# Gate weights' low parts on GpSimd, the scan lane at 2 steps a tick, and the last quarter of the late modulation beside the output projection

## The chip, the cores and the metric

One core of a Trainium2 chip runs the whole program. The metric is the time of one execution on the device in microseconds (us). Of the core's engines this case speaks of PE (TensorE, matmuls), DVE (VectorE), ACT (ScalarE), POOL (GpSimd) and SP (SyncE, which issues most of the DMAs).

## What is computed

One layer of a latent-token backbone: 512 tokens of width 2048, 256 context tokens, all in float32. The conditioning vector c gives six modulation rows of 2048 each, by a matrix-vector product. Cut to what this case touches:

```python
mod_lat = silu(c) @ w_mod + b_mod
sh1, sc1, g1, sh2, sc2, g2 = split(mod_lat, 6)          # six blocks of 2048
h = modulate(x, norm1_w, sh1, sc1)
z = h @ w_in                                             # 2048 -> 1024 + 1024 + 2*2048
y_a = s5_branch(z[:, :1024], ...)                        # state-space scan, readout, w_glu
y_b = pool_branch(z[:, 1024:2048], ...)
gate_a = sigmoid(z[:, 2048:4096]); gate_b = sigmoid(z[:, 4096:6144])
x = x + g1 * ((gate_a * (y_a @ proj_a) + gate_b * (y_b @ proj_b)) @ w_out)
x = x + g2 * peer_ffn(modulate(x, norm2_w, sh2, sc2), ...)
out = rmsnorm(x, final_w)
```

The state-space branch works on 64 groups of 16 channels with 64 states each; its scan over chunks of tokens is followed by a readout that multiplies the states by tables made from the parameters.

## The kernel before, in words

**Matmuls in three passes.** A float32 weight block of 128 x 1024 (a chunk) is loaded into `wraw` by SP, rounded to `whi` by ACT (L125), and the remainder `wlo = wraw - whi` is taken by DVE or GpSimd (L126, in `wload`); `mm3` then issues hi x hi, lo x hi and hi x lo (L110 to L112). The pool of `wlo` has two buffers, those of `wraw` and `whi` three. Of a matmul, `psg` is a gate's accumulator, `psp` a projection's, `psr` the readout's, `psl` the late modulation's.

**The order.** The program is written stage by stage, and a scheduler puts each engine's instructions into one fixed order by priority and by when it reckons their inputs to be there; `wload` asks for a high priority. On the chip each engine then runs its own list in order. Side work comes in through *lanes*: generators of small steps. Every `wload` ends in a `tick`, which runs so many steps of each lane as its rate says (3.4 steps a tick for a rate of 3.4). `drain` runs what is left of a lane.

**The stages around the change**, in the time of the profiled execution: the pooling branch with the first four gate_a blocks, up to 546 us; **gates** (546 to 983), 64 chunks of 24 matmuls (8 x (4 chunks of gate_b and 2 of proj_b), then 4 x 4 chunks of gate_a); **readout** and w_glu (983 to 1096); proj_a and merge (1096 to 1194); w_out (1194 to 1375); then the expert layer, with its query matmul (1394 to 1590), dense U (1590 to 2850) and dense V (2850 to 3967).

**Lanes in gates.** Three run beside the gate matmuls:
- `s5_scan` (L672 on), 86 steps of four dependent DVE instructions on 128 x 128 tiles (`sa`, `sb`, `sa`, `B`; L678 to L681) and 8 steps of three copies (L687 to L689). Readout needs all of `B`.
- `s5_m3` (L606 to L622), 32 steps of six GpSimd instructions on 128 x 256 tiles (`m`, `m3t`), each step followed by an SP DMA of the result to a table in HBM (`m3d`); every second step begins with a DMA of `par` and a GpSimd instruction `npar`. All its tiles have one buffer. Readout loads the tables, four steps to each of its eight blocks (`rm`).
- `mod_late` (L804 on), the four modulation blocks that are needed only after the merge, in 16 pieces of 512 columns (four quarters of four pieces; the fourth quarter is g2, which only the very last residual needs). A piece is 16 loads of a 128 x 512 block `lw` (256 KB each, by SP), 16 DVE instructions into `lacc` (L817, L819), then a sum over partitions on PE (`psl`, L824, recorded as a pair of matmuls), an addition on DVE (`lrow`, L825), and a GpSimd DMA into `modd` (L826). The b_mod row comes by a GpSimd DMA too (L822).

GpSimd's list in gates also holds the DMAs that write the gates' results (`mbd`, L771; `sad`, L781). In readout GpSimd multiplies `ru` (L864), eight times, ahead of `ry`, the transposes `pst` and w_glu.

Of the kernel before, what the change touches and what calls it, by code (L numbers as in the profile page):

```python
# [6 lines left out]
F32 = mybir.dt.float32  # L7
# [10 lines left out]
P = 128  # L18
# [75 lines left out]
class Builder:  # L94
# [62 lines left out]
    def body(self, es):  # L157
        tc, nc, I = self.tc, self.nc, self.I
        pool = lambda **k: tc.tile_pool(**k)
        const = es.enter_context(pool(name="const", bufs=1))  # L160
        self.const = const
        self.dram = es.enter_context(pool(name="scr", bufs=1, space=DRAM))
        self.pse = pse = self.es()
        psT = [pse.enter_context(pool(name=f"psT{j}", bufs=1, space=PSUM)) for j in range(2)]
        self.psM, self.psT2 = psT[1], Turns(psT)
        self.psT = self.psT2
        self.psA = pse.enter_context(pool(name="psA", bufs=6, space=PSUM))

        def cload(name, shape, dt=F32):
            t = const.tile(shape, dt, name=name)  # L170
            nc.sync.dma_start(t, I[name])
            return t

        self.ident = cload("ident", [P, P])
        self.ones = const.tile([P, P], F32, name="ones")
        nc.vector.memset(self.ones, 1.0)
        self.epsb = const.tile([P, 1], F32, name="epsb")
        nc.vector.memset(self.epsb, EPS)
        cT = cload("cT", [P, KT, 2])
        self.bmodT = cload("bmodT", [P, 32])  # L180
        self.n1T = cload("n1T", [P, KT])
        self.sil = const.tile([P, KT, 2], F32, name="sil")
        nc.scalar.activation(self.sil, cT, AF.Silu)

        self.bgT = cload("bgT", [P, 8])
        self.kT = cload("kT", [P, 2, P])
        self.iota = cload("iota", [P, P])
        self.lanes = []
        ws = self.es()
        self.wraw = ws.enter_context(pool(name="wraw", bufs=3))  # L190
        self.wlo = ws.enter_context(pool(name="wlo", bufs=2))
        self.whi = ws.enter_context(pool(name="whi", bufs=3))
        self.mixers()
        self.tail()
        self.peer()
        ws.close()
        pse.close()
# [62 lines left out]
    def rstd(self, pool, x, junk):  # L260
        nc = self.nc
        ss = pool.tile([P, 1], F32, tag="ss", name=self.nm("ss"))
        nc.scalar.activation(junk, x, AF.Square, accum_out=ss)
        sd = pool.tile([P, 1], F32, tag="sd", name=self.nm("sd"))
        nc.scalar.activation(sd, ss, AF.Sqrt, bias=self.epsb, scale=1.0 / D)
        rs = pool.tile([P, 1], F32, tag="rs", name=self.nm("rs"))
        nc.vector.reciprocal(rs, sd)
        return rs

    def mixers(self):  # L270
        tc, nc, I = self.tc, self.nc, self.I
        pool = lambda **k: tc.tile_pool(**k)
# [107 lines left out]
        with self.es() as s6:  # L380
            yb, lane_s = self.pool_branch(s6, es_b, hlat, s5, lane_i)
            lane_m = self.lane(0.7, [self.s5_toeplitz(), self.s5_m3()])
            lane = self.lane(3.4, [self.mod_late()])
            self.gates(hlat, yb)
        es_h.close()
        self.drain(lane_s)
        self.drain(lane_m)
        self.check("gates")
        with self.es() as s7:
            gt = self.s5_readout(s7)  # L390
            self.drain(lane)
            es_b.close()
            es_m = self.es()
            m = self.merge(s7, es_m, gt)
        self.m, self.es_m = m, es_m
# [298 lines left out]
    def pool_branch(self, es, es_b, hlat, s5, lane_i):  # L694
        tc, nc, I = self.tc, self.nc, self.I
        pool = lambda **k: tc.tile_pool(**k)
# [4 lines left out]
        with self.es() as s:  # L701
            ptl = ybl
            uss = []
            for nb in range(2):
# [3 lines left out]
                for kb in range(KT // 2):  # L708
                    w = self.wchunk(I["w_in"], kb * 2, 2, W + nb * 512, 512)
# [9 lines left out]
            self.drain(lane_i)  # L719
            s5.close()  # L720
            self.scp = es_b.enter_context(pool(name="scan", bufs=2, side="right"))
            lane_s = self.lane(4, [self.s5_scan()])
            zp = s.enter_context(pool(name="zp", bufs=1, side="right"))
            wm = zp.tile([P, 4, P], F32, name="wm")
            with tc.high_priority(offset=100):
# [57 lines left out]
    def gate(self, hlat, c0):  # L783
        ps = [self.psA.tile([P, 512], F32, tag="acc", name=self.nm("psg")) for _ in range(2)]
        for kb in range(KT // 4):
            w = self.wchunk(self.I["w_in"], kb * 4, 4, c0, 256)
            for kk in range(4):
                k = kb * 4 + kk
                for j in range(2):
                    self.mm3(ps[j], w[:, kk, j * P:(j + 1) * P], hlat[:, k, :], k == 0, k == KT - 1)  # L790
        return ps

    def proj(self, wap, y, c0):
        ps = [self.psA.tile([P, 512], F32, tag="acc", name=self.nm("psp")) for _ in range(2)]
        for kb in range(2):
            w = self.wchunk(wap, kb * 4, 4, c0, 256)
            for kk in range(4):
                k = kb * 4 + kk
                for j in range(2):
                    self.mm3(ps[j], w[:, kk, j * P:(j + 1) * P], y[:, k, :], k == 0, k == 7)  # L800
        return ps


    def mod_late(self):  # L804

        nc, es = self.nc, self.es()
        lp = es.enter_context(self.tc.tile_pool(name="late", bufs=4, side="right"))
        N = 512
        for q, blk in ((0, 2), (2, 4), (1, 3), (3, 5)):
            for n in range(D // N):  # L810
                c0 = blk * D + n * N
                acc = lp.tile([P, N], F32, tag="lacc", name=self.nm("lacc"), bufs=1)
# [12 lines left out]
                nc.vector.tensor_tensor(row[:, 0], row[:, 1], ps[0:1, :], op=OP.add)  # L825
                nc.gpsimd.dma_start(self.modd[:, q * D + n * N:q * D + (n + 1) * N], row[:, 0])  # L826
                yield
        es.close()

    def brow(self, pool, ap, name):  # L830

# [5 lines left out]
    def s5_readout(self, es):  # L837
# [6 lines left out]
        gl = gp.tile([P, 8, SEQ], F32R, name="gl")  # L844
        with self.es() as s:

            s.enter_context(pool(name="pad", bufs=1)).tile([P, 4096], F32, name="pad")
            ryp = s.enter_context(pool(name="ry", bufs=2))
            rb = s.enter_context(pool(name="rb", bufs=2))
            for gb in range(NGB):  # L850
                ch = slice(gb * P, (gb + 1) * P)
                with tc.high_priority(offset=60):
                    U = rb.tile([P, GB, NCL], F32, tag="rU", name=self.nm("rU"))
                    nc.sync.dma_start(U, self.ud[:, gb * GB:(gb + 1) * GB])
                    T = rb.tile([P, Q, P], F32, tag="rT", name=self.nm("rT"))
                    nc.sync.dma_start(T, self.td[:, :, ch])
                    m3 = rb.tile([P, 4, 2, Q, H, 2], F32, tag="rm3", name=self.nm("rm3"))
                    nc.sync.dma_start(m3.rearrange("p b r s h g -> p b (r s h g)"), self.m3d[gb * 4:gb * 4 + 4].rearrange("b p n -> p b n"))
                    u = ryp.tile([NCL, Q, P], F32, tag="ru", name=self.nm("ru"))
                    nc.sync.dma_start(u, self.zs[CTX:NTOK, ch].rearrange("(c t) n -> c t n", t=Q))  # L860
                    dsk = rb.tile([NCL, P], F32, tag="rd", name=self.nm("rd"))
                    nc.sync.dma_start(dsk, I["s5_d"][0:1, ch].broadcast_to([NCL, P]))
# [533 lines left out]
```

## Time and profile before

| | us |
|---|---|
| median of three runs | 3971.0 (3961.94 to 3975.03) |
| the profiled execution | 3968.97, its span 3966.9 |
| PE busy in the span | 3750.0 (95%) |
| DVE busy | 2561.8 (65%) |
| GpSimd busy | 1761.6 (44%) |

All times in the rows are microseconds from the start of the span of that one execution; it took 2 us less than the median. PE is busy nearly everywhere, so stages are compared by what PE loses in each. In a row by stage the busy times are those of PE, PEld (weight loads), DVE, ACT and POOL, in this order. A row of a group of instructions gives their number, their busy time and mean, and the time that the engine stood idle ahead of them with what ended it.

### The profile page before, as it was taken

What the parts mean: (1) busy time and instruction counts of PE and PEld (TensorE: products, weight loads), DVE (VectorE), ACT (ScalarE), POOL (GpSimd) and SP (SyncE); (2) the same over time, 40 slices, a digit from 0 to 9 for tenths busy, and PEclk for the clock granted to TensorE, in tenths of its full rate; (3) what the DMA queues carried; (4) which work ended last, traced back from release to release, by engine and by line L of the source; (5) the groups of instructions that cost most, each with busy time, mean ns of one, the idle gap of its engine ahead of it and who ended that gap; (6) DMA issues with size and microseconds to landing.
All of it is one profiled execution on the core that took longest, in us unless ns stands there. A gap on an engine that the chain in (4) does not pass through costs nothing. (4 is left out here: it accounts for less than half of the span.)

```text
span 3966.9 us, 49308 instructions
## 1 busy us (share of the span) xinstructions
PE 3750.0 (95%) x18841; PEld 3196.8 (81%) x18841; DVE 2561.8 (65%) x3331; ACT 1187.9 (30%) x1752; POOL 1761.6 (44%) x997
## 2 busy tenths in 40 slices
PE   5999998889899899899999999999999999999997
PEld 3478876667777778799999999989977887788886
DVE  4364379996563368986767767655666666665664
ACT  4223331112222222333333333323332333333332
POOL 0043115552322323354444444446555666576652
PEclk8999999999999999999999999999999999999999
DMA  8635658789875422477877778778887877887773
GB/s 269 207 124 186 206 166 231 227 227 302 235 233 175 138 70 91 136 263 281 290 272 267 288 273 291 256 289 290 312 300 279 316 285 281 287 318 282 282 277 123
DMA packets 456382, 954.40 MB, mean 241 GB/s; under 512 B 104721, under 2 KB 248465, under 8 KB 421073
## 3 DMA queue, kind: packets, MB, share of 16 engines
q1 hardware_dynamic: 380320, 584.58, 45.5%
q0 software_dynamic: 46464, 301.03, 20.4%
q10 hardware_dynamic: 29360, 65.64, 4.5%
q8 instruction: 147, 2.41, 0.2%
q14 instruction: 91, 0.74, 0.1%
HBM read 859.88 MB, written 94.93 MB: 241 GB/s over the span
## 5 line engine op out<-in xcount | busy, mean ns | idle before, releaser
L125 ACT CAST whi<-wraw 128x1024 fp32r<-128x1024 f32 x712 | 747.2, 1051 | 1825.2 <-PE psU L111 542.1
L126 POOL TENSOR_TENSOR wlo<-wraw,whi 128x1024 fp32r<-128x1024 f32 x284 | 773.4, 2724 | 946.8 <-ACT whi L125 714.4
L126 DVE TENSOR_TENSOR wlo<-wraw,whi 128x1024 fp32r<-128x1024 f32 x428 | 595.7, 1392 | 591.9 <-ACT whi L125 341.8
L112 PE MATMUL psU<-h2Th,wlo 128*128 128x384 f32 x2048 | 693.6, 339 | 31.7 <-DVE wlo L126 20.0
L110 PE MATMUL psU<-h2Th,whi 128*128 128x384 f32 x2048 | 700.4, 342 | 6.5 <-ACT whi L125 6.5
L111 PE MATMUL psU<-h2Tl,whi 128*128 128x384 f32 x2048 | 692.5, 338 | 0.0
L111 PE MATMUL psV<-wlo,ah 128*128 128x512 f32 x1536 | 607.7, 396 | 10.0 <-POOL wlo L126 5.0
L112 PE MATMUL psV<-whi,al 128*128 128x512 f32 x1536 | 607.0, 395 | 0.0
L110 PE MATMUL psV<-whi,ah 128*128 128x512 f32 x1536 | 558.0, 396 | 9.5 <-DVE ffn L1233 5.2
L112 PEld LDWEIGHTS psU<-h2Th,wlo 128*128 128x128 f32 x2048 | 387.2, 189 | 35.9 <-issue 14.2
L1096 DVE SCALAR_TENSOR_TENSOR row<-row,h 128x2048 f32<-128x2048 f32 x128 | 340.9, 2663 | 90.2 <-DMA row<-in_u,eid 90.2
L110 PEld LDWEIGHTS psU<-h2Th,whi 128*128 128x128 f32 x2048 | 389.0, 190 | 8.4 <-ACT whi L125 8.1
L111 PEld LDWEIGHTS psU<-h2Tl,whi 128*128 128x128 f32 x2048 | 388.0, 189 | 0.0
L1089 DVE SCALAR_TENSOR_TENSOR ffn<-row,w,ffn 128x2048 f32<-128x2048 f32 x127 | 357.7, 2816 | 13.5 <-DMA row<-in_v,eid 13.5
L111 PEld LDWEIGHTS psV<-wlo,ah 128*128 128x128 f32 x1536 | 290.8, 189 | 80.7 <-POOL wlo L126 8.2
L110 PEld LDWEIGHTS psV<-whi,ah 128*128 128x128 f32 x1536 | 290.9, 189 | 77.4 <-issue 10.3
L112 PEld LDWEIGHTS psV<-whi,al 128*128 128x128 f32 x1536 | 290.3, 189 | 67.6
L1081 POOL DMA_INDIRECT row<-in_u,eid x128 | 206.2, 1611 | 249.7 <-ACT w L1097 76.6
L1144 DVE TENSOR_TENSOR oh<-io,iT 128x512 bf16<-128x512 bf16 x192 | 168.9, 920 | 193.1 <-PE psd L1152 193.0
L1081 POOL DMA_INDIRECT row<-in_v,eid x128 | 241.0, 1883 | 19.1 <-issue 6.6
L819 DVE SCALAR_TENSOR_TENSOR lacc<-lw,sil,lacc 128x512 f32<-128x512 f32 x240 | 213.6, 890 | 52.1 <-DMA lw<-in_w_mod 50.1
L112 PE MATMUL psg<-hhi,wlo 128*128 128x512 f32 x512 | 205.0, 405 | 25.9 <-DVE wlo L126 25.8
(349 smaller groups left out, 5600.4 us busy)
## 6 DMA issues: line engine op xcount, KB each, us to landing
wraw<-in_uT SPq DMA_DIRECT2D x256, 512.0 KB, 5.2
wraw<-in_v SPq DMA_DIRECT2D x256, 512.0 KB, 6.2
lw<-in_w_mod SPq DMA_DIRECT2D x256, 256.0 KB, 4.3
wraw<-in_w_in SPq DMA_DIRECT2D x96, 512.0 KB, 4.8
wmod<-in_w_mod SPq DMA_DIRECT2D x48, 512.0 KB, 5.1
sd<-sev ACTq DMA_DIRECT2D x64, 384.0 KB, 6.0
gds<-ast ACTq DMA_DIRECT2D x12, 2048.0 KB, 8.8
sr<-sd SPq DMA_DIRECT2D x32, 768.0 KB, 7.2
```

The costliest lines, as they stand in the source:

```text
L110: mm(ps, a.hi, b.hi, start=start, stop=False)
L111: mm(ps, a.hi, b.lo, start=False, stop=False)
L112: mm(ps, a.lo, b.hi, start=False, stop=stop)
L125: nc.scalar.copy(hi, raw)
L126: ins = (eng or nc.vector).tensor_tensor(lo, raw, hi.bitcast(F32), op=OP.subtract)
L819: nc.vector.scalar_tensor_tensor(acc, w, self.sil[:, k, 0:1], acc, op0=OP.mult, op1=OP.add)
L1081: nc.gpsimd.indirect_dma_start(out=r, out_offset=None, in_=I[tab], in_offset=bass.IndirectOffsetOnAxis(ap=eid[:, k:k + 1], axis=0))
L1089: V.scalar_tensor_tensor(acc, v, w, acc, op0=OP.mult, op1=OP.add)
L1096: V.scalar_tensor_tensor(u, u, 1.0, h2, op0=OP.mult, op1=OP.mult, accum_out=w[:, 0:1])
L1144: V.tensor_tensor(oh[:, q], self.io4, iT[:, q, ts].unsqueeze(1).broadcast_to([P, P, NT]), op=OP.is_equal)
```

## The change

Four edits, three of them to lanes:
1. In gates (not in the four gate_a blocks before it) `wload` is given GpSimd for the 64 subtractions `wlo`, by `self.gate_lo`.
2. The scan lane gets 2 steps a tick instead of 4.
3. `mod_late` takes a list of quarters. Three quarters run as before, at 2.6 steps a tick instead of 3.4. The fourth runs as a second generator, `late2`, in a pool of its own with two `lw` buffers instead of four, started when w_glu begins, at 1.3 a tick through w_glu, proj_a and w_out, and drained after `tail`. To make room the pad in readout shrinks.
4. Readout, which loads no weights, gets two ticks per block.

```diff
+        self.drain(self.lane_g2)
+        self.es_g2.close()
         self.peer()
...
-            lane = self.lane(3.4, [self.mod_late()])
+            lane = self.lane(2.6, [self.mod_late("late", "right", ((0, 2), (2, 4), (1, 3)))])
+            self.gate_lo = nc.gpsimd
             self.gates(hlat, yb)
+            self.gate_lo = None
...
+        self.es_g2 = self.es()
+        late2 = self.mod_late("late2", "left", ((3, 5),))
+        next(late2)
         with self.es() as s7:
             gt = self.s5_readout(s7)
             self.drain(lane)
             es_b.close()
+            self.lane_g2 = self.lane(1.3, [late2])
...
-            lane_s = self.lane(4, [self.s5_scan()])
+            lane_s = self.lane(2, [self.s5_scan()])
...
-            w = self.wchunk(self.I["w_in"], kb * 4, 4, c0, 256)
+            w = self.wchunk(self.I["w_in"], kb * 4, 4, c0, 256, self.gate_lo)
...
-            w = self.wchunk(wap, kb * 4, 4, c0, 256)
+            w = self.wchunk(wap, kb * 4, 4, c0, 256, self.gate_lo)
...
-    def mod_late(self):
-
-        nc, es = self.nc, self.es()
-        lp = es.enter_context(self.tc.tile_pool(name="late", bufs=4, side="right"))
+    def mod_late(self, name, side, parts):
+
+        nc = self.nc
+        es = self.es() if side == "right" else self.es_g2
+        lp = es.enter_context(self.tc.tile_pool(name=name, bufs=4 if side == "right" else 2, side=side))
         N = 512
-        for q, blk in ((0, 2), (2, 4), (1, 3), (3, 5)):
+        if side == "left":
+            yield
+        for q, blk in parts:
...
-            s.enter_context(pool(name="pad", bufs=1)).tile([P, 4096], F32, name="pad")
+            s.enter_context(pool(name="pad", bufs=1)).tile([P, 1536], F32, name="pad")
...
             for gb in range(NGB):
                 ch = slice(gb * P, (gb + 1) * P)
+                self.tick()
+                self.tick()
```

What it does to the lists of the engines is shown in three places. A row has the line, the operation, and what it writes and reads; lines of the changed kernel are 10 to 16 higher than those of before.

GpSimd's list in the first part of gates, before: m3 steps with a few DMAs between them.

```order
L608 TENSOR_SCALAR npar_4831<-par_805_4829 128x64
L617 TENSOR_TENSOR m3t_4834<-pm_4380,par_805_4829 128x256
L616 TENSOR_TENSOR m_807_4833<-pm_4380,par_805_4829 128x256
L619 TENSOR_TENSOR m_807_4833<-pm_4380,npar_4831 128x256
L618 TENSOR_TENSOR m_807_4833<-m_807_4833,m3t_4834 128x256
L826 DMA modd<-lrow_4979 16x1x32
L620 TENSOR_TENSOR m3t_4834<-pm_4380,par_805_4829 128x256
L621 TENSOR_TENSOR m_807_4833<-m_807_4833,m3t_4834 128x256
L771 DMA mbd<-sg_5095 128x512
```

The same place in the changed kernel:

```order
L630 TENSOR_TENSOR m3t_4818<-pm_4341,par_762_4700 128x256
L631 TENSOR_TENSOR m_788_4817<-m_788_4817,m3t_4818 128x256
L126 TENSOR_TENSOR wlo_5351<-wraw_5349,whi_5350 128x1024
L781 DMA mbd<-sg_5279 128x512
L781 DMA mbd<-sg_5283 128x512
L618 TENSOR_SCALAR npar_4876<-par_799_4874 128x64
L627 TENSOR_TENSOR m3t_4879<-pm_4341,par_799_4874 128x256
L126 TENSOR_TENSOR wlo_5406<-wraw_5404,whi_5405 128x1024
L626 TENSOR_TENSOR m_801_4878<-pm_4341,par_799_4874 128x256
L629 TENSOR_TENSOR m_801_4878<-pm_4341,npar_4876 128x256
L628 TENSOR_TENSOR m_801_4878<-m_801_4878,m3t_4879 128x256
L126 TENSOR_TENSOR wlo_5467<-wraw_5465,whi_5466 128x1024
```

A wlo stands after every two or three m3 instructions, behind whatever mbd, modd and npar stand ahead of it.

DVE's list between the third and the fourth psl, before: lacc, scan and wlo in turn.

```order
L819 SCALAR_TENSOR_TENSOR lacc_5366<-lw_5373,sil,lacc_5366 128x512
L678 TENSOR_TENSOR sa_4958<-ar_256,B 128x128
L679 TENSOR_TENSOR sb_4959<-ai_257,B 128x128
L126 TENSOR_TENSOR wlo_5556<-wraw_5554,whi_5555 128x1024
L819 SCALAR_TENSOR_TENSOR lacc_5366<-lw_5432,sil,lacc_5366 128x512
L680 TENSOR_TENSOR sa_4958<-sa_4958,sb_4959 128x128
L819 SCALAR_TENSOR_TENSOR lacc_5366<-lw_5435,sil,lacc_5366 128x512
L681 TENSOR_TENSOR B<-B,sa_4958 128x128
L819 SCALAR_TENSOR_TENSOR lacc_5366<-lw_5438,sil,lacc_5366 128x512
```

Just ahead of the third psl in the changed kernel:

```order
L832 SCALAR_TENSOR_TENSOR lacc_5011<-lw_5322,sil,lacc_5011 128x512
L690 TENSOR_TENSOR sa_5661<-sa_5661,sb_5662 128x128
L832 SCALAR_TENSOR_TENSOR lacc_5011<-lw_5367,sil,lacc_5011 128x512
L691 TENSOR_TENSOR B<-B,sa_5661 128x128
L688 TENSOR_TENSOR sa_5715<-ar_256,B 128x128
L689 TENSOR_TENSOR sb_5716<-ai_257,B 128x128
L690 TENSOR_TENSOR sa_5715<-sa_5715,sb_5716 128x128
L691 TENSOR_TENSOR B<-B,sa_5715 128x128
```

The wlo are gone. The second lacc row is the last of its piece; behind it five whole scan steps stand one after the other before the next lrow.

GpSimd's list at the end of gates and the start of readout, in the changed kernel:

```order
L631 TENSOR_TENSOR m_1155_6509<-m_1155_6509,m3t_6510 128x256
L618 TENSOR_SCALAR npar_6628<-par_1181_6626 128x64
L627 TENSOR_TENSOR m3t_6631<-pm_6446,par_1181_6626 128x256
L626 TENSOR_TENSOR m_1183_6630<-pm_6446,par_1181_6626 128x256
L629 TENSOR_TENSOR m_1183_6630<-pm_6446,npar_6628 128x256
L628 TENSOR_TENSOR m_1183_6630<-m_1183_6630,m3t_6631 128x256
L835 DMA lrow_8889<-in_b_mod 1x16x32
L791 DMA sad<-sg_7755 128x512
L630 TENSOR_TENSOR m3t_6631<-pm_6446,par_1181_6626 128x256
L791 DMA sad<-sg_7758 128x512
L880 TENSOR_TENSOR ru_7807<-ru_7807,rd_7809 64x1024
L880 TENSOR_TENSOR ru_7874<-ru_7874,rd_7876 64x1024
```

Before, the eight ru (L864) stand there one after the other, right behind the last two sad:

```order
L781 DMA sad<-sg_7920 128x512
L781 DMA sad<-sg_7923 128x512
L864 TENSOR_TENSOR ru_7950<-ru_7950,rd_7952 64x1024
L864 TENSOR_TENSOR ru_8002<-ru_8002,rd_8004 64x1024
L864 TENSOR_TENSOR ru_8054<-ru_8054,rd_8056 64x1024
```

The last steps of m3, which before end well ahead of the end of gates, now reach into readout, ahead of ru and between them.

## Rows read from the trace of the kernel before

**Rows 1.** Busy time by stage: stretch, length, engines with instructions, granted clock, DMA share, GB/s.

```profile
546.00:983.00 437.00, 388.01 (x1561) 296.91 (x1559) 387.59 (x655) 81.89 (x92) 203.24 (x257) 0.95 0.83 244
983.00:1096.00 113.00, 100.12 (x626) 87.05 (x625) 59.22 (x73) 29.61 (x37) 34.34 (x20) 0.92 0.82 238
1096.00:1194.00 98.00, 95.04 (x407) 74.86 (x406) 65.63 (x81) 28.49 (x37) 29.65 (x19) 1.00 0.72 234
1194.00:1375.00 181.00, 180.22 (x772) 143.82 (x770) 56.18 (x55) 43.73 (x60) 46.77 (x42) 1.00 0.47 158
```

**Rows 2.** Timeline of PE, two matmuls 17 apart: start, duration, engine, line, operation.

```profile
945.82 0.39 PE L112 MATMUL psg<-hhi,wlo 128*128 128x512 f32 x1
...
949.67 0.39 PE L111 MATMUL psg<-hlow,whi 128*128 128x512 f32 x1
```

**Rows 3.** Timeline of PE, the first, seventh and tenth psl.

```profile
585.51 1.87 PE L824 MATMUL psl<-lacc,ones 128*1 128x512 f32 x2 [3.54 <-DVE lacc L819]
...
804.28 1.86 PE L824 MATMUL psl<-lacc,ones 128*1 128x512 f32 x2
...
924.07 1.02 PE L824 MATMUL psl<-lacc,ones 128*1 128x512 f32 x2 [0.50 <-DVE lacc L819]
```

**Rows 4.** Waits of PE in gates: us in total, times, longest.

```profile
PE psg L112 <- DVE wlo L126: 25.8, 15, 5.6
```

**Rows 5.** DVE's groups in gates; of the scan's four lines the longest and shortest.

```profile
L819 DVE SCALAR_TENSOR_TENSOR lacc<-lw,sil,lacc 128x512 f32<-128x512 f32 x185 | 165.5, 895 | 35.1 <-DMA lw<-in_w_mod 33.9
L126 DVE TENSOR_TENSOR wlo<-wraw,whi 128x1024 fp32r<-128x1024 f32 x64 | 83.2, 1299 | 4.9 <-ACT whi L125 4.2 <-PE psg L112 0.6
L678 DVE TENSOR_TENSOR sa<-ar,B 128x128 f32<-128x128 f32 x84 | 38.6, 459 | 1.0
...
L679 DVE TENSOR_TENSOR sb<-ai,B 128x128 f32<-128x128 f32 x84 | 28.0, 333 | 0.0
```

**Rows 6.** Timeline of DVE in gates, with GpSimd busy (two) and without (three).

```profile
651.41 1.19 DVE L819 SCALAR_TENSOR_TENSOR lacc<-lw,sil,lacc 128x512 f32<-128x512 f32 x1
652.52 0.82 DVE L678 TENSOR_TENSOR sa<-ar,B 128x128 f32<-128x128 f32 x1
...
655.86 0.74 DVE L819 SCALAR_TENSOR_TENSOR lacc<-lw,sil,lacc 128x512 f32<-128x512 f32 x1
656.52 0.28 DVE L681 TENSOR_TENSOR B<-B,sa 128x128 f32<-128x128 f32 x1
656.73 0.74 DVE L819 SCALAR_TENSOR_TENSOR lacc<-lw,sil,lacc 128x512 f32<-128x512 f32 x1
```

**Rows 7.** Timeline of GpSimd at the same time.

```profile
651.42 0.64 POOL L620 TENSOR_TENSOR m3t<-pm,par 128x256 f32<-128x256 f32 x1
652.13 1.07 POOL L621 TENSOR_TENSOR m<-m,m3t 128x256 f32<-128x256 f32 x1
```

**Rows 8.** GpSimd's groups in gates; of m3's six lines the longest and shortest.

```profile
L621 POOL TENSOR_TENSOR m<-m,m3t 128x256 f32<-128x256 f32 x32 | 31.6, 989 | 2.5
...
L617 POOL TENSOR_TENSOR m3t<-pm,par 128x256 f32<-128x256 f32 x32 | 24.4, 764 | 1.0
```

**Rows 9.** GpSimd's groups in the query matmul (1394 to 1590 us).

```profile
L126 POOL TENSOR_TENSOR wlo<-wraw,whi 128x1024 fp32r<-128x1024 f32 x28 | 67.5, 2409 | 129.2 <-PE psq L112 129.2
```

**Rows 10.** Timeline of GpSimd and DVE in dense U, around two wlo of DVE.

```profile
1668.61 3.31 POOL L126 TENSOR_TENSOR wlo<-wraw,whi 128x1024 fp32r<-128x1024 f32 x1 [1.38 <-ACT whi L125]
1669.58 3.43 DVE L126 TENSOR_TENSOR wlo<-wraw,whi 128x1024 fp32r<-128x1024 f32 x1
...
1679.40 1.22 DVE L126 TENSOR_TENSOR wlo<-wraw,whi 128x1024 fp32r<-128x1024 f32 x1
```

**Rows 11.** Waits of GpSimd in gates: us in total, times, longest.

```profile
POOL npar L608 <- DMA par<-in_s5bc: 78.8, 16, 13.2
POOL m L616 <- DMA m3d<-m: 45.4, 18, 5.7
POOL modd L826 <- DVE lrow L825: 34.2, 8, 14.2
```

More of the change, by code (lines that the diff above doesn't have):

```diff
@@ L268, in rstd @@
         return rs
+    gate_lo = None
     def mixers(self):
@@ L827, in mod_late @@
                 yield
-        es.close()
+        if side == "right":
+            es.close()
     def brow(self, pool, ap, name):
```

## The prediction

> **What bounds the kernel now.** I read the busy time of each engine by stage first [rows 1]. The change touches the gates stage (546 to 983 us) and the three stages behind it. In gates PE is busy 388 of 437 us and DVE 388 too, at a granted clock of 0.95. In the two matmul stages that receive the moved quarter PE is full (95 of 98, 180 of 181) while DVE has room (66 and 56 us busy). So the one place with something to win is gates: what PE loses there.
>
> PE's own floor in gates: full-rate matmuls start 17 apart in 3.85 us, 0.2265 us each [rows 2]; a weight chunk has 24 of them, 5.45 us, and 64 chunks need 349 us. With 12 pairs of psl (about 1 us a pair, 1.9 at a lower clock [rows 3]) that is some 362 us of 437. The remaining 75 us are what a perfect change could give. PE's waits name wlo on DVE, 25.8 us ahead of psg alone [rows 4]. So DVE decides, or rather where DVE is in its fixed order when PE asks for a wlo or a lacc.
>
> Why DVE is full: the lines of DVE in gates [rows 5] beside single instructions [rows 6]. A lacc step takes 0.74 us when nothing is beside it and 895 ns on the mean; a scan instruction 0.28 undisturbed and about 0.40 on the mean of its four lines (333 to 459 ns, 337 instructions). At 651 to 653 us the cause is visible [rows 6, 7]: lacc takes 1.19, sa 0.82 and GpSimd's m 1.07 (0.64 for the instruction ahead of it), ending one after the other. DVE and GpSimd hold each other up when both read two SBUF tiles. The sum: 185 x 0.155 + 337 x 0.12 + 64 x 0.08 = 29 + 40 + 5 = 74 us, caused by 192 m3 instructions (six lines of 32, the dearest and the cheapest in [rows 8]): **0.385 us of DVE per m3 instruction**, 60% of its undisturbed 0.64.
>
> **The change part by part.**
>
> *Low parts to GpSimd.* DVE loses 64 wlo of 1.22 us. GpSimd gets them at 2.41 us each where it runs beside little else [rows 9]: 154 us on an engine that is busy 203 of 437. Some 40 of the m3 instructions (0.76 to 0.99 us over the six lines, about 0.86 [rows 8]) then come after the last wlo, so its total in gates is about 203 + 154 - 40 x 0.86 = 323 us: not the bound by itself. What a wlo on GpSimd costs DVE is not to be seen in gates before; the nearest row is in dense U, where one on GpSimd from 1668.61 stretches DVE's wlo from 1.22 to 3.43 us [rows 10]: 2.2 us when DVE has work waiting. The low bound is the share that m3 costs, 60% of 2.41, 1.4 us. Both are more than the 1.15 to 1.22 that DVE saves. A lower price is not excluded where DVE idles; that is the first rival. I take 1.75 us for the first part of the stage, where DVE is hardly ever without work.
>
> The Trainium skill ("SBUF — State Buffer", section "Who interferes with whom") speaks against this part: a DVE instruction with two SBUF inputs and a GpSimd instruction that reads SBUF exclude each other for the whole instruction. The 3.43 us row agrees. By that rule at full price (2.41 a wlo, 0.64 an m3) step 2 below would take 275 us instead of 240; the gates' 0.385 per m3 says that only some of it reaches DVE.
>
> *The scan lane, 4 to 2 steps a tick.* The rate falls, but the order of DVE does not spread: the scan's last copy stands before the seventh psl now, and stood behind the ninth before. Between psl 1 and psl 7 there are now 66 scan steps (264 instructions) and 24 copies where there were 55 steps and 1 copy, beside the same 96 lacc steps. So the room that the wlo leave is filled with scan, early, and the end of the stage is empty for DVE.
>
> *The last quarter.* psl 1 to 12 lay in gates before, 1 to 10 do now: 2 x 16 lacc steps of 0.74 to 0.9, about 26 us of DVE, leave the end of gates, and their lw loads (0.25 MB each) a stretch with a DMA share of 0.83.
>
> *The sum by psl marks*, since PE waits there for DVE in order. Before: psl 1 at 585.5, psl 7 at 804.3, psl 10 at 924.1 us [rows 3].
> 1. To psl 1: 6 to 7 wlo hold DVE for 9 to 14 us, and its own queue is 2 us shorter: 592 to 600, I take 596.
> 2. psl 1 to 7 (29.2 chunks; PE alone 29.2 x 5.45 + 6 = 165). DVE undisturbed: a lacc to the next start 0.66, a scan instruction 0.21, more where it needs the one ahead, mean 0.27 [rows 6]; 96 x 0.66 + 264 x 0.27 + 24 copies and 14 small additions at about 0.5 = 63 + 71 + 20 = 154. Locks: 79 m3 x 0.385 = 30; 29 wlo x 1.4 to 2.2 = 41 to 64. Waits for lw: 0 to 17 (half of the 33.9 in [rows 5]). Together 225 to 265; I take 240. The same working for before gives 63 + 220 x 0.27 + 30 wlo x 1.15 + 10 + 37 for half of the m3 + 17 = 221, against 218.8 measured.
> 3. psl 7 to 10 (12.8 chunks): DVE 41 + 13 wlo x 1.4 to 2.2 + 27 m3 x 0.385 = 69 to 80; PE 73. I take 77.
> 4. psl 10 to the end (15.5 chunks): PE 84.5; GpSimd 16 x 2.41 + 36 m3 x 0.86 + 13 small ones at 0.6 = 77, nearly as much, before any wait. I take 92 (85 to 100).
>
> Sum 596 + 240 + 77 + 92 = 1005, against 983: **gates +22** (-8 to +64).
>
> *GpSimd's queue* is in order, and now wlo stand behind m3, modd and npar, and PE behind wlo. Before, m waited 45.4 us for m3d (18 times), npar 78.8 for par (16), modd 34.2 for DVE's lrow (8), with nobody urgent behind them [rows 11]. Two wlo buffers give a lead of one chunk, 5.45 us, of which the wlo itself takes 2.4, so a wait of over 3 us just ahead of a wlo shows on PE. Where DVE sets the pace (8 us a chunk in step 2) there is room for it; in step 4 there is not, which is why I take 92 there. The rest is a rival.
>
> *Readout.* About 40 m3 instructions stand ahead of, and between, the eight ru. The first ru waits for some 14 of them, 12 us after the last wlo. PE has the first block's psr and part of the next first (about 45 short matmuls, 10 us), so 0 to 3 us show; the last blocks' m3 are hidden under w_glu matmuls that now stand among the psr groups. With that cover gone it would be 40 x 0.86 = 34 us. psl 11 to 13 and two extra ticks a block fill some of PE's gaps (13 of 113 us). Net 0 (-8 to +12).
>
> *proj_a and w_out.* psl 15 and 16 go from proj_a to w_out, with two lw buffers instead of four, at a DMA share of 0.47. DVE's lacc steps lie in its 125 us of room there. PE is full in both, so a late lacc costs at once: +2 (0 to 6). The peer stages keep their order but for a few rows: 0.
>
> Total +24. The profiled execution is 3968.97 us, 2 below the median of 3971.0: 3993 in its terms, **3995** in the median's (+0.6%).
>
> **Rivals.**
>
> *DVE is relieved, faster.* If a wlo on GpSimd costs DVE well under 1.15 us, PE's pace decides: 349 + 10 psl + 20 to 35 us left of its 75 lost ones, 380 to 395 us of gates, 42 to 57 less: 3915 to 3958, with the middle at 3925. For it: m3 costs only 60% of its length, DVE idles 34 us on lw, and two lacc sets leave. Against it: the 3.43 us row, and the scan, packed ahead of psl 7. By steps 2 to 4 the stage breaks even at about 1.2 us a wlo with the lw waits gone.
>
> *It cancels, same.* A price of 1.1 to 1.4, or 10 us given back in readout: 3960 to 3982, at 3971.
>
> *GpSimd's queue stalls PE, slower.* 13 npar, 10 modd and 25 m stand among the wlo. 23 x 4.6 us = 106 us if all of the first two reach PE; a third of them, 35 us, on top of the 22: 4030. For it: par, m and m3t have one buffer each, so these waits are real latencies. Against it: often a wlo stands between, and hides 2.4 us of one. It decides once they pass the 3 us of lead at most wlo.
>
> **How the numbers follow.** The forecast (lock price 1.4 to 2.2) has 0.45, its own range 3972 to 4033; relieved 0.25; cancelled 0.20; queue stalls 0.10. The range leaves out the better half of the relieved case (0.13) and the worse half of the last (0.05): 3938 to 4030. Within 0.3% (12 us, about what a measurement of this kernel tells from no change): 0.22, with the forecast's lowest edge; faster 0.25; slower 0.53.
>
> **What would show it.** In the new profile psl 7 should lie at 822 to 860 us and the last matmul of gates at about 1005; lacc and scan instructions between psl 1 and 7 should be longer than before (over 1.0 and 0.45 us on the mean); a wlo on GpSimd should take 2.7 to 3.2 us; PE should wait for lacc at psl. After psl 7 PE should run at 5.5 to 6 us a chunk. If lacc falls towards 0.75 and psl 7 stands before 790, the price of the lock was wrong and the kernel is faster. If PE's waits name GpSimd's wlo for over 40 us, the queue rival is right. A gain or loss of over 10 us behind the readout would be wrong in every case here.

## The result, and the profile after

The changed kernel is slower: 4061.4 us median (4060.44 to 4070.67) against 3969.61 us of the kernel before, ratio 1.0234, 95% interval 1.0213 to 1.0255. The prediction had the sign (3995 us, +0.6%) and a quarter of the size; the measured time lies 31 us above the top of its range. The profiled execution is the longest of the four, 4070.67 us with a span of 4068.9, so the differences by stage below add up to 102 us where the medians differ by 92.

Busy time by stage after the change, in the columns of [rows 1] (stretch, length, PE, PEld, DVE, ACT, POOL, granted clock, DMA share, GB/s): gates up to the last gate matmul, readout with w_glu, proj_a, w_out. Line numbers are those of the changed kernel.

```profile
546.00:1063.00 517.00, 402.55 (x1589) 308.43 (x1588) 393.14 (x575) 84.82 (x97) 309.15 (x283) 0.89 0.67 195
1063.00:1202.00 139.00, 110.41 (x632) 92.19 (x631) 81.27 (x95) 31.50 (x41) 62.01 (x57) 0.88 0.84 233
1202.00:1292.00 90.00, 89.30 (x385) 71.09 (x384) 57.92 (x67) 27.34 (x34) 29.42 (x18) 1.00 0.76 240
1292.00:1477.00 185.00, 182.08 (x773) 143.60 (x772) 72.68 (x69) 43.04 (x58) 48.85 (x45) 1.00 0.53 168
```

Before, the last gate matmul lay at 983 us and w_glu ended at 1101 (not at 1096, the boundary in [rows 1]). So gates are 80 us longer (517 against 437), readout with w_glu 21 (139 against 118), proj_a 3 shorter, w_out 5 longer, and all that follows 1 shorter. In gates DVE is busy 393 us, as long as before (388), although 64 wlo and two lacc pieces have left it; GpSimd is busy 309 instead of 203; the DMA share falls from 0.83 to 0.67, and PE's granted clock from 0.95 to 0.89, with PE waiting more.

PE's waits in gates after the change (us in total, times, longest):

```profile
PE psl L837 <- DVE lacc L832: 52.0, 9, 12.1
PE psg L112 <- POOL wlo L126: 44.4, 13, 11.9
PE psg L110 <- ACT whi L125: 14.4, 3, 7.2
PE psp L112 <- POOL wlo L126: 3.5, 2, 1.8
```

These are 114 us. Before they were 48.9; beside the 25.8 in [rows 4] there were:

```profile
PE psp L112 <- DVE wlo L126: 16.7, 8, 4.0
PE psl L824 <- DVE lacc L819: 6.4, 5, 3.5
```

So the wait for lacc, that is for a DVE that comes late, grew by 46 us, and a wait for whi of 14 us is new. The waits for wlo are about as long as before (47.9 against 42.5 us) and name another engine. These are 65 of the 80 us; the other 15 are PE's own busy time (403 against 388 us), at the lower granted clock. DVE's groups in the same stretch, to be held against [rows 5] (mean ns behind the comma):

```profile
L832 DVE SCALAR_TENSOR_TENSOR lacc<-lw,sil,lacc 128x512 f32<-128x512 f32 x165 | 190.6, 1155 | 58.6 <-DMA lw<-in_w_mod 56.6
L690 DVE TENSOR_TENSOR sa<-sa,sb 128x128 f32<-128x128 f32 x86 | 53.0, 616 | 1.5
...
L689 DVE TENSOR_TENSOR sb<-ai,B 128x128 f32<-128x128 f32 x85 | 41.2, 485 | 0.0
```

A lacc step went from 895 to 1155 ns, the scan's four lines from 333 to 459 up to 485 to 616. GpSimd's wlo takes 2.52 us on the mean there:

```profile
L126 POOL TENSOR_TENSOR wlo<-wraw,whi 128x1024 fp32r<-128x1024 f32 x64 | 161.1, 2518 | 38.7 <-DVE ybl L136 23.2 <-ACT whi L125 7.8 <-issue 3.9
```

One place shows what goes wrong. GpSimd's timeline from 698 us, then DVE's behind it, then the PE matmul that waits, then what SP issued and ACT rounded for it (start, duration, and in brackets the idle time ahead and what ended it):

```profile
698.41 2.84 POOL L126 TENSOR_TENSOR wlo<-wraw,whi 128x1024 fp32r<-128x1024 f32 x1
709.30 0.59 POOL L781 DMA_DIRECT2D mbd<-sg  x1 [8.05 <-DVE sg L780]
710.76 0.54 POOL L781 DMA_DIRECT2D mbd<-sg  x1 [0.87 <-DVE sb L689]
715.53 0.37 POOL L618 TENSOR_SCALAR npar<-par 128x64 f32<-128x64 f32 x1 [4.22 <-DMA par<-in_s5bc]
...
716.46 2.78 POOL L126 TENSOR_TENSOR wlo<-wraw,whi 128x1024 fp32r<-128x1024 f32 x1
...
721.23 2.81 POOL L126 TENSOR_TENSOR wlo<-wraw,whi 128x1024 fp32r<-128x1024 f32 x1
```

```profile
716.97 2.42 DVE L690 TENSOR_TENSOR sa<-sa,sb 128x128 f32<-128x128 f32 x1
...
721.74 2.45 DVE L689 TENSOR_TENSOR sb<-ai,B 128x128 f32<-128x128 f32 x1
```

```profile
719.30 1.22 PE L112 MATMUL psg<-hhi,wlo 128*128 128x512 f32 x2 [11.86 <-POOL wlo L126]
```

```profile
702.09 3.12 SPq L828 DMA_DIRECT2D lw<-in_w_mod  x4
705.26 0.42 SPq L124 DMA_DIRECT2D wraw<-in_w_in  x1
...
711.52 1.04 ACT L125 CAST whi<-wraw 128x1024 fp32r<-128x1024 f32 x1 [14.59 <-DMA wraw<-in_w_in]
```

First the lock: a scan instruction of 0.28 us takes 2.42 beside the wlo of 716.46, and another 2.45 beside the next one, at 721.23. Then the wlo that came late, for which PE stood 11.86 us from 707.4 on. Its weights came late: SP issued the load at 705.26, behind lw loads that wait for DVE to free their buffers (in gates SP's lw loads wait some 250 us in all for DVE, before 140), and whi was ready only at 712.56. That is 5.1 us of the wait. Then the queue: an npar that waited for par held the wlo until 716.46, 3.9 us. The rest is the wlo itself. The two mbd that waited for sg were gone by 711.3, ahead of whi, and cost nothing here.

### The profile page after: what moved, and what is told of

The parts are those of the page before. It is cut to its first block, busy times and chain, and to the rows that moved or that the text cites. A ratio compares the mean times of both kernels' runs of the same rounds, so it can differ in the third digit from the quotient of the medians.

```text
span 4068.9 us, 49271 instructions
## 1 busy us (share of the span) xinstructions
PE 3776.3 (93%) x18841; PEld 3208.1 (79%) x18841; DVE 2588.4 (64%) x3267; ACT 1185.3 (29%) x1752; POOL 1895.2 (47%) x1061
## 3 DMA queue, kind: packets, MB, share of 16 engines
q8 instruction: 148, 2.42, 0.2%
## 5 line engine op out<-in xcount | busy, mean ns | idle before, releaser
L126 POOL TENSOR_TENSOR wlo<-wraw,whi 128x1024 fp32r<-128x1024 f32 x348 | 938.7, 2698 | 976.3 <-ACT whi L125 724.5
L126 DVE TENSOR_TENSOR wlo<-wraw,whi 128x1024 fp32r<-128x1024 f32 x364 | 513.7, 1411 | 605.8 <-ACT whi L125 320.0
L1105 DVE SCALAR_TENSOR_TENSOR ffn<-row,w,ffn 128x2048 f32<-128x2048 f32 x127 | 340.8, 2683 | 21.2 <-DMA row<-in_v,eid 21.2
L832 DVE SCALAR_TENSOR_TENSOR lacc<-lw,sil,lacc 128x512 f32<-128x512 f32 x240 | 263.0, 1097 | 117.0 <-DMA lw<-in_w_mod 114.1
L1097 POOL DMA_INDIRECT row<-in_v,eid x128 | 228.3, 1783 | 19.9 <-issue 7.4
```

Of the source, the lines that this page charges most:

```text
L126: ins = (eng or nc.vector).tensor_tensor(lo, raw, hi.bitcast(F32), op=OP.subtract)
L832: nc.vector.scalar_tensor_tensor(acc, w, self.sil[:, k, 0:1], acc, op0=OP.mult, op1=OP.add)
L1097: nc.gpsimd.indirect_dma_start(out=r, out_offset=None, in_=I[tab], in_offset=bass.IndirectOffsetOnAxis(ap=eid[:, k:k + 1], axis=0))
L1105: V.scalar_tensor_tensor(acc, v, w, acc, op0=OP.mult, op1=OP.add)
```

## Experiments

Theory 1 is the lock: while a wlo runs on GpSimd, DVE cannot run an instruction with two inputs in SBUF. Its rivals are theory 2, that the new order and the moved quarter cost the time, and theory 3, that wlo come late because GpSimd's queue is long and waits. A gates end is the start of the last gate matmul.

### The changed kernel with wlo back on DVE

```diff
-            self.gate_lo = nc.gpsimd
+            self.gate_lo = None
```

> The changed kernel with one part undone: the gates' wlo go back to DVE; the scan lane, the moved quarter and the ticks in readout stay. Theory 1 (a wlo on GpSimd locks DVE out for 2.2 us): nearly all of the loss goes; lacc in gates averages 0.85 to 0.95 us again, a PE chunk takes about 6.6 us up to the seventh psl, gates end at 960 to 980 us, total 3940 to 3965 us, a little under the kernel before since two lacc pieces have left gates. Theory 2 (the loss is the new order: scan packed early, quarter moved, ticks): gates still end past 1030 and the total stays above 4030 us.

Measured: 3971.76 us, ratio to the kernel before 1.0016 (1.0004 to 1.0028). Gates end at 982 us, readout with w_glu takes 130, proj_a 90, w_out 186. So the loss is the wlo on GpSimd, and theory 2 falls. A miss all the same: the total lies 7 us above the expected range, and gates did not get shorter although two lacc pieces left them. The scan's last copy lies at 868 us here, as in the whole change (867; before at 906): the early scan and the pieces that left gates come to nothing together. No run parts the two.

### The kernel before with the wlo of gates on GpSimd

```diff
+    gate_lo = None
...
+            self.gate_lo = nc.gpsimd
             self.gates(hlat, yb)
+            self.gate_lo = None
...
-            w = self.wchunk(self.I["w_in"], kb * 4, 4, c0, 256)
+            w = self.wchunk(self.I["w_in"], kb * 4, 4, c0, 256, self.gate_lo)
...
-            w = self.wchunk(wap, kb * 4, 4, c0, 256)
+            w = self.wchunk(wap, kb * 4, 4, c0, 256, self.gate_lo)
```

> The kernel before with one part added: the 64 wlo of gates on GpSimd, nothing else. Theory 1 (lock): slower than the whole change, since 11 or 12 lacc pieces stay in gates: psl 1 to 7 takes about 255 to 275 us, gates end at 1060 to 1085 us, total 4060 to 4095 us. Theory 2 (order and lanes): within 25 us of the kernel before, 3960 to 3995 us.

Measured: 4059.91 us, ratio 1.0243 (1.0226 to 1.026), gates end at 1065. This one edit makes the whole loss; the other three, in sum, neither add to it nor take from it. PE's waits in gates (us in total, times, longest):

```profile
PE psl L828 <- DVE lacc L823: 73.2, 11, 16.0
PE psg L112 <- POOL wlo L126: 32.1, 13, 5.2
```

With the lacc pieces left in gates PE waits still more for lacc, as the lock has it. But psl 1 to 7 takes 245 us (586 to 831), not the 255 to 275 expected, and the total lies at the lower edge of its range.

### The changed kernel with wlo that read nothing

```diff
-            ins = (eng or nc.vector).tensor_tensor(lo, raw, hi.bitcast(F32), op=OP.subtract)
+            if eng is nc.gpsimd and self.gate_lo is not None:
+                ins = eng.memset(lo.bitcast(F32), 0.0)
+            else:
+                ins = (eng or nc.vector).tensor_tensor(lo, raw, hi.bitcast(F32), op=OP.subtract)
```

> The changed kernel, in which GpSimd's 64 wlo of gates are each one instruction that fills the tile with zeros and reads nothing (so the low parts of the gate weights are left out of the result). They keep their place behind GpSimd's m3, modd and npar, but hold no port for reading, if that is what blocks. Theory 1 (the lock of reads): the lacc and scan instructions are stretched by m3 alone, lacc 0.85 to 0.95 us on the mean, no scan instruction over 2 us, gates end at 945 to 975 us, total 3930 to 3965 us. Theory 3 (GpSimd's queue: wlo late behind its waits for m3d, par and lrow): PE still waits over 40 us for GpSimd's wlo, gates end past 1010, total over 4005 us.

Measured, in a single execution: 3953.63 us, gates end at 966, w_glu at 1097. lacc takes 861 ns on the mean, as with all wlo on DVE (865), where m3 alone is beside it. GpSimd's timeline, then DVE's:

```profile
666.05 0.95 POOL L127 MEMSET wlo<- 128x1024 f32 x1
```

```profile
666.29 0.29 DVE L691 TENSOR_TENSOR sa<-ar,B 128x128 f32<-128x128 f32 x1
666.50 0.28 DVE L692 TENSOR_TENSOR sb<-ai,B 128x128 f32<-128x128 f32 x1
```

A fill of the same tile does not touch DVE's two-input instructions. But it is also 1.5 us shorter than the subtraction, so the next one was needed.

### The same with three fills

```diff
+                eng.memset(lo.bitcast(F32), 1.0)
+                eng.memset(lo.bitcast(F32), 2.0)
                 ins = eng.memset(lo.bitcast(F32), 0.0)
```

> The changed kernel with each of GpSimd's 64 wlo of gates replaced by three instructions that fill the tile and read nothing, 3 x 0.95 = 2.86 us by the run with one of them: GpSimd is held longer than by the real wlo (2.41 us), its queue is as long or longer, but nothing of it reads (the low parts of the gate weights are left out of the result). Theory 1 (the lock of reads): DVE is stretched by m3 alone, lacc 0.85 to 0.95 us on the mean and scan instructions about 0.40; gates end at 960 to 1000 us, total 3950 to 3995 us, the excess over the run with one fill being the price of the queue alone. Theory 3 (the queue): the time that GpSimd is occupied is what counts, gates end past 1030 us, total over 4025 us, PE waits over 70 us for GpSimd's wlo.

Measured, in a single execution: 3988.01 us, gates end at 1015, w_glu at 1130; the total as theory 1 expects, gates past its 1000. lacc stays at 872 ns. PE's waits:

```profile
PE psg L112 <- POOL wlo L129: 38.0, 17, 6.0
PE psl L842 <- DVE lacc L837: 13.6, 4, 7.2
PE psp L112 <- POOL wlo L129: 12.8, 6, 3.4
```

GpSimd is held longer here than by the real wlo (64 x 2.9 us), and PE waits 51 us for it (42 with one fill), but 14 for lacc. Against the single fill gates lose 49 us. Not all of this is lost: 68 short matmuls of readout (9 us) stand ahead of the last gate matmul here, none with one fill and 18 in the changed kernel, and readout with w_glu takes 115 us instead of 131. So the runs are compared at the end of w_glu, where all of them have the same part of the program behind them: 1097 us with one fill, 1130 with three, 1202 with the real wlo. By these marks GpSimd's time and queue, without reading, cost 33 us (34 by the totals), and the real wlo another 72 (73 by the totals). The 72 us are the reading, but also its wait: a fill needs no whi, and with the real wlo SP cannot load the next wraw before it (47 us of waits in gates). No run parts this from the lock. The scheduler also put the psl closer together here (every four chunks up to the seventh, where the changed kernel has nearly five on the mean), so the two shares are good to some 10 us, not better.

### m3 taken out, before and after

```diff
-                Gp.tensor_tensor(m3[:, 0], er, c_, op=OP.mult)
...
-                Gp.tensor_tensor(m3[:, 1], m3[:, 1], tmp, op=OP.subtract)
+                Gp.memset(m3, 0.0)
```

In the kernel before:

> The kernel before with the six m3 instructions of each of the 32 steps replaced by one that fills the tile with zeros (the readout tables are left out of the result). It measures what m3 costs DVE, which the prediction put at 0.385 us an instruction, 74 us in all. Theory 1: lacc falls to 0.74 to 0.78 us on the mean and scan instructions to 0.28 to 0.32; gates get shorter by 30 to 50 us (the rest of the 74 was slack), total 3918 to 3940 us. If DVE's means stay as they are, m3 and the lock are not what stretches them, and the total stays within 12 us of 3970.

Measured, in a single execution: 3921.6 us, gates end at 934. DVE's groups in gates:

```profile
L814 DVE SCALAR_TENSOR_TENSOR lacc<-lw,sil,lacc 128x512 f32<-128x512 f32 x177 | 133.0, 752 | 68.9 <-DMA lw<-in_w_mod 67.3
...
L673 DVE TENSOR_TENSOR sa<-ar,B 128x128 f32<-128x128 f32 x83 | 23.8, 287 | 1.2
L674 DVE TENSOR_TENSOR sb<-ai,B 128x128 f32<-128x128 f32 x83 | 23.4, 282 | 0.0
```

So 752 and 282 to 287 ns are DVE's undisturbed times, m3 is what stretches them before, and it costs the kernel before 49 us of gates, of which 35 are left at the end of w_glu (1066 against 1101 us).

In the changed kernel:

> The changed kernel with the six m3 instructions of a step replaced by one fill (the readout tables are left out of the result): GpSimd's queue holds the real wlo and little else, and its waits for m3d and par get shorter or lie beside nothing. The companion is the kernel before without m3, 3921.6 us with gates to 934 us. Theory 1 (lock by wlo, 2.2 us each where DVE has work): scan instructions and lacc are still stretched, by 60 to 100 us in sum; psl 7 at 815 to 835 us; gates end 20 to 40 us later than the companion's, total 3942 to 3970 us. Theory 3 (wlo late behind m3 and its waits): without m3 the loss is gone, total 3910 to 3935 us.

Measured, in a single execution: 3961.3 us, gates end at 979.5, 45 us behind the companion, and psl 7 lies at 838; both are somewhat later than expected. At the end of w_glu it is 36 us behind (1103 against 1066), in total 40: without m3 the changed kernel still loses some 40 of the 90 us that the wlo on GpSimd cost with it (the companion lacks the other three edits too). GpSimd's queue is not empty, it still waits for m3d and par, and PE waits 37 us in gates for wlo. But m3 no longer reads beside DVE. GpSimd's timeline, then DVE's:

```profile
702.36 0.53 POOL L626 MEMSET m<- 128x512 f32 x1 [1.50 <-DMA m3d<-m]
702.85 2.34 POOL L126 TENSOR_TENSOR wlo<-wraw,whi 128x1024 fp32r<-128x1024 f32 x1
```

```profile
702.70 0.29 DVE L683 TENSOR_TENSOR sa<-ar,B 128x128 f32<-128x128 f32 x1
702.91 2.43 DVE L684 TENSOR_TENSOR sb<-ai,B 128x128 f32<-128x128 f32 x1
705.38 0.29 DVE L685 TENSOR_TENSOR sa<-sa,sb 128x128 f32<-128x128 f32 x1
```

DVE's groups between its first and seventh psl (591 to 838 us), and GpSimd's:

```profile
L827 DVE SCALAR_TENSOR_TENSOR lacc<-lw,sil,lacc 128x512 f32<-128x512 f32 x90 | 85.4, 949 | 10.4 <-DMA lw<-in_w_mod 9.5
L683 DVE TENSOR_TENSOR sa<-ar,B 128x128 f32<-128x128 f32 x70 | 33.4, 476 | 1.5
...
L684 DVE TENSOR_TENSOR sb<-ai,B 128x128 f32<-128x128 f32 x70 | 26.9, 384 | 0.0
```

```profile
L126 POOL TENSOR_TENSOR wlo<-wraw,whi 128x1024 fp32r<-128x1024 f32 x34 | 83.0, 2441 | 7.5 <-PE psg L112 3.8 <-PE psp L112 3.6
```

90 x (0.949 - 0.74) = 19 for lacc; the scan's four lines have a mean of 0.44, 280 x 0.16 = 45; its copies add some 8. Together 72 us by 34 wlo, an estimate of **2.1 us each**: nearly the whole length of a wlo, where DVE has work waiting.

### Half of the wlo

```diff
+        if self.gate_lo is not None:
+            self.turn = not self.turn
+            eng = self.gate_lo if self.turn else None
...
+    turn = False
```

> The changed kernel with every second wlo of gates back on DVE, so 32 on each. Theory 1 (each wlo on GpSimd costs DVE 2.2 us and saves it 1.15): half of the loss against the run with all on DVE, 4005 to 4030 us, lacc and scan stretched by about 120 us in sum. Theory 3 (GpSimd's queue is only too long when it has all of them): GpSimd's total falls to some 270 us of 440, no loss is left, 3960 to 3985 us.

Measured: 4002.54 us, ratio 1.0093 (1.0057 to 1.0128), gates end at 1016. Half of the wlo make a third of the loss over all on DVE (31 of 90 us), a little under the range expected of the lock; the threshold of theory 3 is not there either.

### Only the last 16 chunks

```diff
-            self.gate_lo = nc.gpsimd
...
+        self.gate_lo = nc.gpsimd
         for j2 in range(4, 8):
             self.gate_a(hlat, j2)
```

> The changed kernel with GpSimd's wlo only in the last 16 chunks of gates, where the scan is done and DVE has two lacc pieces and little else. Theory 1: the lock costs only where DVE has work waiting; here it costs under 0.7 us a wlo and saves 1.15, so the total stays within 12 us of the run with all wlo on DVE (3960 to 3984 us), and no lasting gain, since PE is the bound there. If a wlo on GpSimd costs the same anywhere (a quarter of the loss), 3990 to 4000 us.

Measured: 3973.13 us, ratio 1.0025 (1.0006 to 1.0044), gates end at 977. With the scan done, the wlo on GpSimd neither cost nor gain anything that can be told from the run with all on DVE.

### mbd and modd issued by SP

```diff
-                nc.gpsimd.dma_start(self.mbd[j2 * 2 + j], sg)
+                nc.sync.dma_start(self.mbd[j2 * 2 + j], sg)
...
-                nc.gpsimd.dma_start(self.modd[:, q * D + n * N:q * D + (n + 1) * N], row[:, 0])
+                nc.sync.dma_start(self.modd[:, q * D + n * N:q * D + (n + 1) * N], row[:, 0])
```

> The changed kernel with the DMAs that write gates' results (mbd) and the late modulation (modd) issued by SP instead of GpSimd, so that GpSimd's wlo no longer stand behind instructions that wait for DVE's sg and lrow (43.8 us of waits in the changed kernel). Theory 1 with 3 (lock and queue add): PE's waits for GpSimd's wlo fall by 10 to 30 us, the lock stays (2 us a wlo), total 4030 to 4055 us. Theory 1 alone: no change over 12 us, 4050 to 4073 us. Should SP, which waits now in GpSimd's stead, hold back wraw and lw, the total goes above 4075 us.

Measured: 4029.96 us, ratio 1.0161 (1.0109 to 1.0212), at the lower edge of the range for lock and queue together; gates end at 1039: 24 us of gates come back. Not where I expected it, though: PE's waits for wlo rise (57 us against 48), those for lacc and whi fall.

```profile
PE psg L112 <- POOL wlo L126: 39.2, 14, 8.9
PE psl L837 <- DVE lacc L832: 38.5, 7, 10.2
PE psp L112 <- POOL wlo L126: 17.7, 6, 4.1
```

The waits in GpSimd's queue are a part of the loss, and the lock stays. By what path they come back as shorter waits for lacc, no run here shows.

### Without wlo on GpSimd and without the ticks in readout

```diff
-            self.gate_lo = nc.gpsimd
+            self.gate_lo = None
...
-                self.tick()
-                self.tick()
```

> The changed kernel with the gates' wlo back on DVE and without the two ticks a block in readout, so that of the change the moved quarter and the scan lane are left. With the ticks, readout and w_glu took 130 us against 118 before, with none of m3 behind the last gate. If the ticks (lacc and lw loads in readout) are the cause, this falls to 116 to 122 us and the total to 3955 to 3967 us, at or under the kernel before. If the moved quarter's loads in w_glu are, readout and w_glu stay at 127 us or more and the total at 3966 to 3980 us.

Measured: 3958.86 us, ratio 0.9982 (0.9963 to 1.0). Readout with w_glu takes 116 us, against 130 with the ticks and 118 before. So the ticks cost 14 us in readout; proj_a is 5 us shorter with them, and by the two ratios to the kernel before they cost 0.34%, some 13 us. The moved quarter and the scan lane without them are worth 0.2% (0 to 0.4). This is the only version of the whole kernel here that is not behind the one before.

## Why the prediction was wrong, step by step

**The mechanism: right.** DVE and GpSimd exclude each other, and a wlo on GpSimd costs DVE more than the 1.15 us that it saves. The m3 price of 0.385 us, read from means in the trace of before, holds: without m3 lacc falls to 752 ns, where 740 was taken for undisturbed, and with the times measured there the price is 0.37. What failed are terms of the sum: steps 2 to 4 and readout were all forecast too small.

**Step 1, psl 1: right** (592.4 us, predicted 592 to 600). The marks after the change:

```profile
592.43 1.86 PE L837 MATMUL psl<-lacc,ones 128*1 128x512 f32 x2 [6.58 <-DVE lacc L832]
...
864.86 1.86 PE L837 MATMUL psl<-lacc,ones 128*1 128x512 f32 x2 [9.76 <-DVE lacc L832]
...
959.28 1.87 PE L837 MATMUL psl<-lacc,ones 128*1 128x512 f32 x2 [6.52 <-DVE lacc L832]
```

Between these marks (columns as above):

```profile
592.00:865.00 273.00, 188.98 (x713) 141.97 (x714) 256.10 (x420) 36.52 (x40) 150.30 (x143) 0.85 0.61 177
865.00:959.00 94.00, 79.87 (x314) 60.61 (x312) 66.20 (x59) 15.63 (x17) 62.83 (x56) 0.90 0.78 235
959.00:1063.00 104.00, 95.98 (x399) 75.68 (x400) 26.31 (x21) 19.00 (x22) 74.55 (x74) 0.95 0.73 210
```

**Step 2, psl 1 to 7: mis-sized**, 272 us against 240 (225 to 265). DVE does set the pace: it is busy 256 of the 273 us. With the forecast's own prices for undisturbed instructions, and 0.385 for each of 84 m3, some 65 us are left for 30 wlo. So a wlo cost 2.1 to 2.2 us, where 1.75 was taken between 1.4 and 2.2. This is the largest part, some 13 of the 32 us. The row at the upper end, the 3.43 us in [rows 10], was the right one; the low end came from the share of m3, but m3 has gaps, while here DVE nearly always had work behind a wlo. Another 12 us are DVE's idle time, 17 us (11 of them on lw) where the forecast left about 5. Some 6 are a wrong count: the 264 scan instructions lie between two lrow, but the marks lie at the last lacc of a piece, and from mark to mark there are 286. The rule of the Trainium skill ("SBUF — State Buffer", section "Who interferes with whom"), at its full price, would have given 275 for this step, by the estimate in the prediction. The trace agrees with it on the wlo: a scan instruction of 0.28 us begun beside one took 2.42. That 275 comes so near 272 is partly luck, since that sum has no idle time of DVE and the short count.

**Step 3, psl 7 to 10: mis-sized**, 94 against 77. DVE is busy 66 us, less than the 74 that the forecast has at its price of 1.75. I left out DVE's waits for lw, though step 2 had a term for them: DVE was idle 57 us on lw in gates after, against 34 before, 23 of them here. Why the loads were so late here is not shown.

**Step 4, to the end: mis-sized**, 104 against 92 (85 to 100). PE's waits in it are 7.7 us (6.4 for wlo, 1.3 for whi), what the forecast allowed; the 6.5 us for lacc lie ahead of psl 10, in step 3. PE itself is busy 96 us where 84.5 were counted at the full clock. The granted clock is 0.95: behind the waits that end at 959.28 and 1019.85 PE runs at the lower level (1.2 GHz) until 963.6 and 1025.0, gate matmuls there starting 0.43 us apart instead of 0.23. And 18 matmuls of readout, 3 us, stand ahead of the last gate matmul. A chunk takes 7.4 us in step 3 and 6.6 in step 4, not the 5.5 to 6 that were to show. (The upper ends of the four steps add up to +62 for gates, not +64.)

**Readout: wrong.** Predicted 0 (-8 to +12), measured +21. The ticks, entered as filling PE's gaps, cost some 14. The rest of the cause is open. The m3 behind the last gate (32 here) are not measured alone: the kernel before with wlo on GpSimd, which has such a tail and no ticks, takes 132 us there instead of 118, but so does the kernel before without m3, which has neither. So the term that I called hidden under w_glu matmuls is neither shown nor refuted.

**proj_a, w_out and behind: right** (+2 together, -1 behind), though the +2 are -3 and +5, so partly luck. In the terms of the profiled execution step 1 gives -4, steps 2 to 4 +32, +17 and +12, readout +21 and the rest -1: 77 of the 78 us between 3993 and 4070.67. No term for the queue is needed beside them.

**The queue rival: its sign came true, but was no sign.** It was to be right if PE's waits named GpSimd's wlo for over 40 us. They do for 47.9, but before PE waited 42.5 us for wlo too, then named DVE's. The rival put a third of the queue's waits on top of the lock, 35 us, with a chance of 0.10. The fills, which hold GpSimd and read nothing, give 33 us for its time and queue and 72 more for the real wlo, less some 15 that DVE's relief gave (1097 against 1112 us at the end of w_glu): the 90 us between 1112 and 1202. So the larger share is the real wlo's own, its reading above all. Whether the 33 come on top of it in the changed kernel is not shown: between psl 1 and 7 PE waits 39 us for wlo, but DVE's work fills that time, as the forecast had it ("Where DVE sets the pace there is room for it"). That GpSimd's waits cost something all the same is shown by mbd and modd on SP, which give 24 us of gates back; by what path is open.

**The scan's order: not shown to cost anything.** That the scan is packed ahead of psl 7 is true. It is as early with the wlo on DVE, where gates end as before; but two lacc pieces have left gates there, and what they gave may have paid for it.

## What to carry to other kernels

An instruction is not moved for free to an idle engine when the two engines exclude each other: look in the trace for one pair of rows that overlap, one on GpSimd and one on DVE, and take the longer duration there as the price wherever DVE has a backlog. Count what stands ahead of a moved instruction in its new queue as a second price (33 us here, for fills that read nothing), and look at what a late engine holds up in other queues, as DVE did with lw and the weight loads behind it. Compare runs at a mark that has the same work ahead of it in all of them: the end of gates was not one, since matmuls of readout slip ahead of it. An edit that puts side work into a stage with gaps (the ticks) is tried by itself: here PE's gaps there were not free.

## What the runs showed of the hardware that was not expected

The hold is sharper than I took it for. It is nearly the whole length of the instruction: a DVE instruction that began 0.06 us behind a GpSimd wlo of 2.34 us took 2.43 instead of 0.28 us. And for two-input instructions reading decides, not occupation: beside fills of 0.95 us, which only write, DVE's instructions of 128 x 128 took 0.28 to 0.29 us.

Two more things are in the traces. GpSimd, then DVE, in the changed kernel:

```profile
859.25 2.78 POOL L126 TENSOR_TENSOR wlo<-wraw,whi 128x1024 fp32r<-128x1024 f32 x1
...
874.19 2.51 POOL L126 TENSOR_TENSOR wlo<-wraw,whi 128x1024 fp32r<-128x1024 f32 x1
```

```profile
859.87 2.45 DVE L699 COPY B<-sw 64x512 f32<-64x512 f32 x1
...
863.14 0.42 DVE L697 COPY sw<-B 64x512 f32<-64x512 f32 x1
...
874.37 1.28 DVE L780 TENSOR_TENSOR sg<-sg,psp 128x512 f32<-128x512 f32 x2
```

The scan's copy, with one input in SBUF, is held as well: 2.45 us instead of 0.42. For copies writing is enough: in the run with three fills a copy begun at 790.08, beside a fill of 1.23 us, took 1.14 us. The two sg, whose second input psp lies in PSUM, take 0.68 us each beside a wlo, as before (677 ns).
